# Squared activations: their sums made on GpSimd after the reload, the residual reloaded in two parts, conditioning loads given queues and slots of their own

## The chip, the cores and the metric

One core of one Trainium2 chip. The metric is the device time of one execution, in microseconds (us). Engines by their names in the profile: PE is TensorE's matmul (PEld its weight load), DVE is VectorE, ACT is ScalarE, POOL is GpSimd, SP is SyncE, whose queue issues nearly all DMAs here.

## The reference

Two transformer-like layers on x of 1024 frames by 1024 channels, fp32. Conditioning vectors come from one vector c:

```python
for layer in range(2):
    mod = silu(c) @ ada_w[layer] + ada_b[layer]          # 6 vectors of 1024
    sh1, sc1, g1, sh2, sc2, g2 = split(mod, 6)
    hn = rms_norm(h) * (1 + sc1) + sh1
    y = recurrent_mixer(hn) if layer == 0 else chunk_attention(hn, k, v)
    h = h + g1 * y
    hn = rms_norm(h) * (1 + sc2) + sh2
    h = h + g2 * (square(relu(hn @ w1)) @ w2)            # 1024 -> 4096 -> 1024
    if layer == 0:
        k, v = shared_kv(h, ...)                         # own shift and scale from c
```

## The kernel before

Activations lie transposed, channels on partitions, 1024 frames in two halves of 512. Every fp32 operand is split into a high part (a rounding copy on ScalarE) and a low part (the difference, on VectorE or GpSimd), and each product takes three matmuls (`mm3`: high by high, high by low, low by high).

The stages in order of time: start and first norm (to about 60 us), the recurrence (tiles t = 1 to 10: projections on PE, a convolution and a scan on VectorE, gates), the output projection of the mixer in three pieces of channels, MLP 0 (up 660 to 900 us, down to 1234 us), queries, keys and values (to 1520 us), attention (to 1740 us), its output projection, MLP 1 (up from about 1920 us, down from about 2180 us to the end).

Both MLPs multiply 2 by 2 blocks with seven products in place of eight (`quad`, `PROD`: B11, T1, T2, B22, T3, B21, T4). The sums of weights are four operations on GpSimd (`sums` in `add_quad`). **Up**: p = 0, 1 are done plainly, then 14 quads p = 2 to 15 of 7 x 4 x 3 = 84 matmuls; each leaves two tiles `ca`, `cb_` with the four squared blocks. `store` makes the sums T1 to T4 of these on VectorE (four operations of 128x512, two more slots) and writes eight blocks to a DRAM tensor `hid`. **Down**: 16 steps (`STEPS`): three small ones over 1, 2 and 3 of the p, then 13 full ones over four. A step needs seven operands of one new p, reloaded from `hid` and split, and four weight blocks. At the end a tail of plain products. Between up and down the residual h (8 tiles of 512 KB) is reloaded.

`Stream` feeds all weights: a list of items in order, each with loads, a split and a place: kind "w" (weights, 8 high or low tiles), kind "a" (reloaded activations, in the pool of 38 general slots) or a `use` (the 128 rows of a conditioning matrix, for which VectorE multiplies by c and sums, L235: 96 of the 112 go through the stream). All items pass one ring of 7 staging tiles `ws`, strictly in order: an item that can't be split yet holds back all behind it. `some(n)` puts n conditioning items into the list. A scheduler orders each engine's instructions in advance.

## Time and profile before

| | us |
|---|---|
| median of 3 runs | 2513.43 (2509.39 to 2513.71) |
| profiled execution, device time | 2512.36 |
| its span, first to last instruction | 2510.6 |
| PE busy | 2328.9 (93%) |
| DVE busy | 1882.3 (75%) |
| ACT busy / POOL busy | 1118.3 / 869.3 |

The device time lies 1.8 us over the span. Busy PE is not PE at its peak: a matmul's record lasts longer than its share of the pipeline, so the count of matmuls in a stretch says more than the busy time.

### The profile page before, as it was taken

What the parts mean: (1) busy time and instruction counts of PE and PEld (TensorE: products, weight loads), DVE (VectorE), ACT (ScalarE), POOL (GpSimd) and SP (SyncE); (2) the same over time, 40 slices, a digit from 0 to 9 for tenths busy, and PEclk for the clock granted to TensorE, in tenths of its full rate; (3) what the DMA queues carried; (4) which work ended last, traced back from release to release, by engine and by line L of the source; (5) the groups of instructions that cost most, each with busy time, mean ns of one, the idle gap of its engine ahead of it and who ended that gap; (6) DMA issues with size and microseconds to landing.
All of it is one profiled execution on the core that took longest, in us unless ns stands there. A gap on an engine that the chain in (4) does not pass through costs nothing.

```text
span 2510.6 us, 31957 instructions
## 1 busy us (share of the span) xinstructions
PE 2328.9 (93%) x11764; PEld 1959.8 (78%) x11764; DVE 1882.3 (75%) x2472; ACT 1118.3 (45%) x1808; POOL 869.3 (35%) x623
## 2 busy tenths in 40 slices
PE   4978997997999979999999999999999999889999
PEld 3656875875777757888899998998787888668887
DVE  8868987679777788887655465998379777777884
ACT  5466764344222234444354216998144333344441
POOL 3434445342222214232111026885044333132330
PEclk9978997998999989999999999999999999989999
DMA  7343235223565585555323400002314444755442
GB/s 292 124 138 117 72 100 180 71 84 130 193 201 191 193 286 182 182 169 189 118 60 111 142 5 12 10 20 77 143 42 151 170 170 165 258 158 160 148 151 92
DMA packets 138221, 342.50 MB, mean 136 GB/s; under 512 B 14064, under 2 KB 19312, under 8 KB 138064
## 3 DMA queue, kind: packets, MB, share of 16 engines
q1 hardware_dynamic: 136768, 336.13, 41.0%
q10 hardware_dynamic: 1296, 4.33, 0.4%
q8 instruction: 92, 1.51, 0.2%
q14 instruction: 65, 0.53, 0.1%
HBM read 244.98 MB, written 83.89 MB: 131 GB/s over the span
## 4 chain that ended last, share of the span: by engine, by line
PE 60%; DVE 19%; DMA 9%; ACT 6%; issue 5%; POOL 0%; SPq 0%; DVEq 0%; ACTq 0%; POOLq 0%
PE b L204 19%; PE b L203 19%; PE b L202 18%; DMA ws<-in_ada_dram 4%; DVE ws L235 3%; DMA ws<-in_kvada_dram 2%; DVE wl L151 2%; PE b L1250 1%; ACT s L1220 1%; DVE s L235 1%; ACT s L207 1%; DVE s L421 1%; DVE s L151 1%; PE b L1269 1%; DMA ws<-in_w_dram 1%
## 5 line engine op out<-in xcount | busy, mean ns | idle before, releaser
L203 PE MATMUL b<-s,wh 128*128 128x512 f32 x2540 | 1014.9, 400 | 57.8 <-DVE s L208 28.6
L202 PE MATMUL b<-s,wh 128*128 128x512 f32 x2540 | 1001.9, 400 | 55.5 <-ACT wh L150 22.6
L204 PE MATMUL b<-s,wl 128*128 128x512 f32 (+1 forms) x2312 | 911.8, 401 | 24.8 <-DVE wl L151 24.6
L203 PEld LDWEIGHTS b<-s,wh 128*128 128x128 f32 x2540 | 487.8, 192 | 177.1 <-DVE s L208 32.5
L202 PEld LDWEIGHTS b<-s,wh 128*128 128x128 f32 x2540 | 486.7, 192 | 175.6 <-ACT wh L150 25.0
L104 POOL TENSOR_TENSOR ws<-ws,ws 128x512 f32<-128x512 f32 (+3 forms) x180 | 290.5, 1614 | 867.6 <-DMA ws<-in_w_dram 448.1
L150 ACT ACTIVATE wh<-ws 128x1024 fp32r<-128x1024 f32 (+4 forms) x324 | 306.3, 946 | 562.9 <-PE b L204 240.8
L204 PEld LDWEIGHTS b<-s,wl 128*128 128x128 f32 (+1 forms) x2312 | 444.9, 192 | 129.5 <-DVE wl L151 31.8
L151 DVE TENSOR_TENSOR wl<-ws,wh 128x1024 fp32r<-128x1024 f32 (+3 forms) x224 | 274.9, 1229 | 143.4 <-PE b L203 72.4
L235 DVE CUSTOM_DVE_ANT_0 ws<-ws,cb,vec 128x1024 f32<-128x1024 f32 x96 | 142.9, 1490 | 158.9 <-DMA ws<-in_ada_dram 125.8
L151 DVE TENSOR_TENSOR s<-ws,s 128x512 fp32r<-128x512 f32 x230 | 193.2, 854 | 40.2 <-ACT s L150 39.8
L202 PE MATMUL b<-wh,s 128*128 128x256 f32 x768 | 217.7, 285 | 3.2 <-ACT s L396 2.0
L203 PE MATMUL b<-wl,s 128*128 128x256 f32 x768 | 217.9, 285 | 0.0
L204 PE MATMUL b<-wh,s 128*128 128x256 f32 x768 | 213.8, 285 | 3.3 <-DVE s L400 3.3
L946 DVE SCALAR_TENSOR_TENSOR s<-b,mod,s 128x512 f32<-128x512 f32 x248 | 181.8, 744 | 45.9 <-PE b L204 44.7
L150 ACT ACTIVATE s<-ws 128x512 fp32r<-128x512 f32 x230 | 138.1, 624 | 137.8 <-PE b L204 80.2
L151 POOL TENSOR_TENSOR wl<-ws,wh 128x1024 fp32r<-128x1024 f32 (+2 forms) x40 | 108.0, 2704 | 224.5 <-ACT wh L150 222.2
L202 PEld LDWEIGHTS b<-wh,s 128*128 128x128 f32 x768 | 148.8, 194 | 3.8 <-ACT s L396 2.3
L204 PEld LDWEIGHTS b<-wh,s 128*128 128x128 f32 x768 | 146.5, 194 | 4.0 <-DVE s L400 3.7
L203 PEld LDWEIGHTS b<-wl,s 128*128 128x128 f32 x768 | 148.8, 194 | 0.2 <-issue 0.2
L1225 POOL TENSOR_SCALAR s<-s,sm 128x640 f32<-128x640 f32 (+4 forms) x128 | 86.2, 685 | 22.1 <-DVE sm L1223 22.0
L104 POOL TENSOR_TENSOR ws<-ws 128x512 f32<-128x512 f32 (+3 forms) x60 | 92.2, 1536 | 0.5 <-DMA ws<-in_w_dram 0.4
(172 smaller groups left out, 3099.7 us busy)
## 6 DMA issues: line engine op xcount, KB each, us to landing
hid<-s SPq DMA_DIRECT2D x128, 512.0 KB
ws<-in_w_dram SPq DMA_DIRECT2D x216, 256.0 KB
ws<-hid SPq DMA_DIRECT2D x96, 512.0 KB
ws<-in_ada_dram SPq DMA_DIRECT2D x80, 512.0 KB
ws<-in_w_in_dram SPq DMA_DIRECT2D x22, 512.0 KB
ws<-hid SPq DMA_DIRECT2D x38, 256.0 KB
s<-in_ada_dram SPq DMA_DIRECT2D x16, 512.0 KB
hsp<-s SPq DMA_DIRECT2D x32, 256.0 KB
```

Of the source, the lines that this page charges most:

```text
L104: G.tensor_tensor(out=out, in0=in0, in1=in1, op=op)
L150: nc.scalar.activation(out=hi[:rows, :n], in_=src, func=AF.Copy)
L151: self.lo_engine.tensor_tensor(out=lo[:rows, :n], in0=src, in1=hi[:rows, :n].bitcast(F32), op=ALU.subtract)
L202: PE.matmul(ps, ah, bh, start=start, stop=False, skip_group_check=more)
L203: PE.matmul(ps, ah, bl, start=False, stop=False, skip_group_check=more)
L204: return PE.matmul(ps, al, bh, start=False, stop=stop, skip_group_check=more).ins
L207: A_.activation(out=hi, in_=src, func=AF.Copy)
L235: V.tensor_tensor_reduce(out=t, in0=t, in1=cb, op0=ALU.mult, op1=ALU.add, scale=1.0, scalar=bias, accum_out=dst)
L421: V.scalar_tensor_tensor(out=t, in0=t, scalar=self.a[:, k : k + 1], in1=self.r[:, hs(half)], op0=ALU.mult, op1=ALU.mult)
L946: V.scalar_tensor_tensor(out=t, in0=ps, scalar=g2[:, m : m + 1], in1=t, op0=ALU.mult, op1=ALU.add)
L1220: A_.activation(out=p[:, lo:640], in_=p[:, lo:640], func=AF.Exp, scale=-1.0, bias=m, accum_out=s1)
L1225: G.tensor_scalar(out=p[:, lo:640], in0=p[:, lo:640], scalar1=sm[:, 4 + e : 5 + e], scalar2=1.0, op0=ALU.mult, op1=ALU.mult)
```

## The change

**Stream**: three queues instead of one order. "w" and "a" each go on in their own order as their places come free; conditioning items are a third kind "u". Loads still stand in one order on SP; a staging tile is now given back when its own item is done, and the sums of weights may run as soon as the four blocks are there, before there is a place for the split.

**Conditioning**: `some(4)` at t = 3 to 8 of the recurrence becomes `some(2)` at t = 3 to 6 (24 items become 8), the output projection takes 16 instead of 8, and 8 move on, into MLP 0's up part, which has its 28 as before, from other vectors; queries to values take 32 instead of 24. The 28 in MLP 0's up part no longer take `ws` tiles but two slots of the general pool (`ada_late`).

**Sums of the activations**: `store` writes only `ca` and `cb_` (4 blocks instead of 8), one quad later. On reload `pair` loads two tiles, and GpSimd makes T3, T1, T2 in place once B11 and B22 are split, and T4 once B21 is.

**Residual**: h tiles 2 to 5 are reloaded during quads 8 to 11, the other four after quad 15. **Start of an MLP**: the low parts of T3 and T4 (8 per layer, `sums` of `NormS`) go from VectorE to GpSimd.

```diff
@@ Stream @@
-        self.loaded = self.split = self.pos = 0
-        self.live = {"w": 0, "a": 0}
-        self.cap = {"w": nh, "a": 0}
+        self.loaded = self.raw = self.pos = 0
+        self.queue = {"w": [], "a": [], "u": []}
+        self.live = {"w": 0, "a": 0, "u": 0}
+        self.cap = {"w": nh, "a": 0, "u": 2}
...
+    def ready(self, it, most):
+        if it["n"] >= self.loaded or (most is not None and it["n"] >= most):
+            return False
+        if it.get("need") is not None and "st" not in it["need"]:
+            return False
+        if it["after"] is not None and it["after"]["at"] < len(it["after"]["ops"]):
+            return False
+        o = it["ops"][it["at"]]
+        return callable(o) or self.live[it["to"]] + (1 if o[2] else 2) <= self.cap[it["to"]]
...
+            self.load(most)
+            for q in self.queue.values():
+                if q and self.ready(q[0], most):
+                    more = True
+                    self.step(q[0])
+                    if q[0]["at"] == len(q[0]["ops"]):
+                        q.pop(0)
@@ conditioning @@
-        some(4 if 2 < t < 9 else 0)
+        some(2 if 2 < t < 7 else 0)
...
-            some(4 if c == 1 and j > 1 else 0)
+            some(2 if c < 2 else 0)
...
-        some(3 if g > 1 else 0)
+        some(4)
@@ operands of MLP down @@
+    def pair(p):
+        x = ws.item([(0, 1024, hid[p][:, 0:2].rearrange("p a b -> p (a b)"))], [])
+        def sub(*ts):
+            def go():
+                a, b = hs(0), hs(1)
+                r0, r1 = x["st"], it["st"]
+                for t in ts:
+                    out, in0, in1 = {3: (r1[:, a], r0[:, b], r1[:, a]),
+                                     1: (r0[:, b], r0[:, b], r0[:, a]),
+                                     2: (r0[:, a], r0[:, a], r1[:, a]),
+                                     4: (r1[:, b], r1[:, b], r0[:, a])}[t]
+                    G.tensor_tensor(out=out, in0=in0, in1=in1, op=ALU.subtract)
+            return go
...
+                     [B11, B22, sub(3, 1, 2), T1, T2, T3, B21, sub(4), T4], to="a", raws=2)
@@ mlp @@
         def store(p, ca, cb_):
-            ta, tb = slot(), slot()
-            a, b = hs(0), hs(1)
-            for out, in0, in1 in ((ta[:, a], ca[:, b], ca[:, a]), (ta[:, b], ca[:, b], cb_[:, a]),
-                                  (tb[:, a], ca[:, a], ta[:, b]), (tb[:, b], cb_[:, b], tb[:, a])):
-                V.tensor_tensor(out=out, in0=in0, in1=in1, op=ALU.subtract)
-            for t, x, d in ((ca, 0, 7), (cb_, 3, 2), (ta, 1, 3), (tb, 2, 4)):
+            for t, x in ((ca, 0), (cb_, 2)):
...
-            def after(w):
+            def after(x):
+                if x == 1 and stored is not None:
+                    store(*stored)
                 if p == 15:
-                    ws.cap["a"] = (4, 8, 16, 30)[w]
+                    ws.cap["a"] = 4 * (x + 1)
                     ws.pump()
             quad([ws.next() for _ in range(4)], 4, nrm.op, read, after)
-            store(p, ca, cb_)
-        h = [slot() for _ in range(KD)]
-        for k in (2, 3, 4, 5, 6, 7, 0, 1):
-            nc.sync.dma_start(h[k], nrm.dram[k])
+            stored = (p, ca, cb_)
+            if p in (8, 9, 10, 11):
+                reload(p - 6)
+        store(*stored)
+        ws.cap["a"] = 30
+        ws.pump()
+        for k in (6, 7, 0, 1):
+            reload(k)
```

What this makes of the order, at three places. VectorE in MLP 0's up part, about one quad, before (L872 the sums of activations, L235 a conditioning multiply, which reads a `ws` tile, L151 a low part, L878 and L924 the reading of products):

```order
L151 TENSOR_TENSOR wl_5299<-ws_5094,wh_5298 128x1024
L872 TENSOR_TENSOR s_5254<-s_5120,s_5253 128x512
L924 TENSOR_TENSOR s_5263<-s_5263,b_5267 128x512
L878 SCALAR_TENSOR_TENSOR s_5263<-s_5263 128x512
L235 ISA ws_5374,kvmod<-ws_5374,cb,vec 128x1024
L235 ISA kvmod 128x1
L928 TENSOR_TENSOR s_5121<-s_5121 128x512
L872 TENSOR_TENSOR s_5254<-s_5121,s_5254 128x512
```

and in the change (L175 the low part, L274 the multiply, L947, L1000 and L1004 the reading of products):

```order
L175 TENSOR_TENSOR wl_5312<-ws_5219,wh_5311 128x1024
L274 ISA s_5349,kvmod<-s_5349,cb,vec 128x1024
L274 ISA kvmod 128x1
L274 ISA s_5352,kvmod<-s_5352,cb,vec 128x1024
L274 ISA kvmod 128x1
L1004 TENSOR_TENSOR s_5146<-s_5146 128x512
L175 TENSOR_TENSOR wl_5345<-ws_5221,wh_5344 128x1024
L1000 TENSOR_TENSOR s_5280<-s_5280,b_5283 128x512
L1000 TENSOR_TENSOR s_5280<-s_5280,b_5284 128x512
```

The sums are gone, the two multiplies of a quad stand together and read general slots. GpSimd in MLP 1's down part, the full steps, before (L104 the sums of weights, four to a step):

```order
L104 TENSOR_TENSOR ws_18997<-ws_19007,ws_18918 128x512
L104 TENSOR_TENSOR ws_18918<-ws_19007 128x512
L104 TENSOR_TENSOR ws_18958<-ws_18997,ws_19007 128x512
L104 TENSOR_TENSOR ws_18958<-ws_18997,ws_18958 128x512
L104 TENSOR_TENSOR ws_19147<-ws_19157,ws_19068 128x512
```

and in the change (L111 the sums of weights, L359 those of activations):

```order
L111 TENSOR_TENSOR ws_18703<-ws_18725,ws_18602 128x512
L111 TENSOR_TENSOR ws_18602<-ws_18725 128x512
L111 TENSOR_TENSOR ws_18666<-ws_18703,ws_18725 128x512
L111 TENSOR_TENSOR ws_18666<-ws_18703,ws_18666 128x512
L359 TENSOR_TENSOR ws_18747<-ws_18728,ws_18747 128x512
L359 TENSOR_TENSOR ws_18728<-ws_18728 128x512
L359 TENSOR_TENSOR ws_18728<-ws_18728,ws_18747 128x512
L359 TENSOR_TENSOR ws_18747<-ws_18747,ws_18728 128x512
L111 TENSOR_TENSOR ws_18853<-ws_18875,ws_18752 128x512
```

A full step has eight operations instead of four. SP's queue where MLP 1 goes from up to down, before (L874 stores, L118 stream loads, L940 the residual):

```order
L874 DMA hid<-s_17923 128x2x512
L940 DMA s_17935<-hsp_15013 128x1024
L940 DMA s_17936<-hsp_15013 128x1024
L940 DMA s_17937<-hsp_15013 128x1024
L940 DMA s_17938<-hsp_15013 128x1024
L940 DMA s_17939<-hsp_15013 128x1024
L874 DMA hid<-s_17768 128x2x512
L940 DMA s_17940<-hsp_15013 128x1024
L940 DMA s_17933<-hsp_15013 128x1024
L874 DMA hid<-s_17924 256x1x512
L940 DMA s_17934<-hsp_15013 128x1024
L118 DMA ws_17968<-hid 128x512
```

and in the change (L944, L137, L987):

```order
L944 DMA hid<-s_17530 128x1024
L137 DMA ws_17755<-hid 128x1024
L137 DMA ws_17769<-hid 128x1024
L137 DMA ws_17777<-in_w_dram 128x512
L987 DMA s_17717<-hsp_14885 128x1024
L987 DMA s_17719<-hsp_14885 128x1024
L987 DMA s_17721<-hsp_14885 128x1024
L987 DMA s_17723<-hsp_14885 128x1024
L137 DMA ws_17806<-in_w_dram 128x512
```

Four of the eight reloads are gone from this place, and they stand behind the operands of the third small step instead of ahead of them. Of the conditioning multiplies ahead of MLP 0, VectorE's order had 24 in the first half of the recurrence and 8 behind; it now has 8 there and then 16, the 16 of the output projection, which are drawn forward into the last four tiles of the recurrence.

## Rows read from the trace of the kernel before

**Rows 1.** The page: its head, and its first part (busy time of each engine, share of the span, instructions).
```profile
span 2510.6 us, 31957 instructions
PE 2328.9 (93%) x11764; PEld 1959.8 (78%) x11764; DVE 1882.3 (75%) x2472; ACT 1118.3 (45%) x1808; POOL 869.3 (35%) x623
```

**Rows 2.** Busy time of each engine by stretch: the stretch and its length, PE, PEld, DVE, ACT, POOL with their instructions, granted clock of PE, DMA share, GB/s.
```profile
60.00:250.00 190.00, 160.19 (x621) 122.17 (x620) 149.60 (x147) 106.61 (x128) 80.84 (x32) 0.87 0.40 124
250.00:480.00 230.00, 211.16 (x868) 165.82 (x867) 195.34 (x137) 142.51 (x157) 113.07 (x40) 0.93 0.36 108
480.00:660.00 180.00, 156.67 (x653) 125.69 (x652) 138.31 (x174) 66.99 (x106) 49.93 (x30) 0.93 0.35 118
660.00:891.00 231.00, 215.24 (x924) 174.51 (x923) 169.04 (x210) 65.86 (x93) 58.17 (x42) 0.99 0.59 194
891.00:960.00 69.00, 53.45 (x207) 40.01 (x206) 57.83 (x85) 25.92 (x45) 16.97 (x14) 0.90 0.84 287
960.00:1234.00 274.00, 273.12 (x1205) 225.11 (x1204) 211.22 (x271) 107.71 (x152) 81.20 (x50) 1.00 0.53 170
1234.00:1520.00 286.00, 279.50 (x2291) 277.95 (x2291) 159.29 (x199) 99.74 (x202) 42.80 (x30) 0.99 0.25 78
1920.00:2162.00 242.00, 242.00 (x1069) 200.37 (x1069) 185.24 (x198) 76.22 (x108) 78.45 (x50) 1.00 0.48 164
2162.00:2220.00 58.00, 42.04 (x147) 31.29 (x145) 43.12 (x62) 19.62 (x35) 12.03 (x11) 0.82 0.77 270
2220.00:2460.00 240.00, 239.59 (x1049) 197.94 (x1050) 194.46 (x230) 101.04 (x141) 82.82 (x50) 0.99 0.50 153
```

**Rows 3.** ACT in order of time, the reading of a quad's last product (L927) of two quads in MLP 0, ten apart, and of two in MLP 1, eleven apart: start, duration, engine and line, idle time before.
```profile
657.56 0.60 ACT L927 ACTIVATE s<-b 128x512 f32<-128x512 f32 x1 [7.94 <-PE b L204]
870.00 0.60 ACT L927 ACTIVATE s<-b 128x512 f32<-128x512 f32 x1 [5.56 <-PE b L204]
...
1931.36 0.60 ACT L927 ACTIVATE s<-b 128x512 f32<-128x512 f32 x1 [3.59 <-PE b L204]
2140.80 0.60 ACT L927 ACTIVATE s<-b 128x512 f32<-128x512 f32 x1 [3.58 <-PE b L204]
```

**Rows 4.** VectorE's waits in 660 to 891 us: who waited for whom, us in total, times, longest.
```profile
DVE ws L235 <- DMA ws<-in_kvada_dram: 32.9, 12, 3.9
DVE ws L235 <- DMA ws<-in_ada_dram: 21.6, 8, 3.0
```

**Rows 5.** The chain that ended last, in order of time, in one quad of MLP 0: start, duration, what.
```profile
718.00 4.75 DMA ws<-in_ada_dram
722.77 1.28 DVE ws L235
724.09 4.17 DMA ws<-in_ada_dram
```

**Rows 6.** VectorE's waits in 60 to 250 us (columns as in rows 4).
```profile
DVE ws L235 <- DMA ws<-in_ada_dram: 31.8, 14, 5.9
```

**Rows 7.** PE's waits in 60 to 250 us.
```profile
PE b L203 <- DVE s L208: 20.6, 4, 11.7
PE b L202 <- ACT s L207: 7.8, 2, 4.0
```

**Rows 8.** PE's waits in 2162 to 2220 us, MLP 1's crossing from up to down.
```profile
PE b L202 <- ACT wh L150: 8.4, 2, 6.0
PE b L204 <- DVE wl L151: 3.9, 2, 3.1
```

**Rows 9.** GpSimd in order of time there: the first sums of weights of the third small step, with the idle time before.
```profile
2198.34 1.01 POOL L104 TENSOR_TENSOR ws<-ws,ws 128x384 f32<-128x384 f32 x1 [17.93 <-DMA ws<-in_w_dram]
```

**Rows 10.** Groups by line with shapes kept apart: line, engine, operation, shapes, count, busy us, mean ns of one, idle before.
```profile
L235 DVE CUSTOM_DVE_ANT_0 ws<-ws,cb,vec 128x1024 f32<-128x1024 f32 x96 | 142.9, 1490 | 158.9 <-DMA ws<-in_ada_dram 125.8 <-DMA ws<-in_kvada_dram 33.0
L872 DVE TENSOR_TENSOR s<-s,s 128x512 f32<-128x512 f32 x96 | 81.6, 850 | 2.0
L872 DVE TENSOR_TENSOR s<-s 128x512 f32<-128x512 f32 x32 | 33.7, 1053 | 0.9
L427 POOL TENSOR_TENSOR s<-s,s 128x512 fp32r<-128x512 f32 x16 | 23.8, 1499 | 34.3 <-ACT s L426 30.0 <-PE b L204 4.4
L444 DVE TENSOR_TENSOR s<-s,s 128x512 fp32r<-128x512 f32 x32 | 22.6, 746 | 0.0
```

**Rows 11.** GpSimd in order of time in one full step of MLP 1's down part, its four sums of weights.
```profile
2323.57 1.76 POOL L104 TENSOR_TENSOR ws<-ws,ws 128x512 f32<-128x512 f32 x1 [13.28 <-DVE s L946]
2325.29 1.29 POOL L104 TENSOR_TENSOR ws<-ws 128x512 f32<-128x512 f32 x1
2326.53 3.54 POOL L104 TENSOR_TENSOR ws<-ws,ws 128x512 f32<-128x512 f32 x2
```

**Rows 12.** VectorE in the same stretch.
```profile
2323.49 0.68 DVE L151 TENSOR_TENSOR s<-ws,s 128x512 fp32r<-128x512 f32 x1
2324.51 0.75 DVE L946 SCALAR_TENSOR_TENSOR s<-b,mod,s 128x512 f32<-128x512 f32 x1 [0.33 <-PE b L204]
2327.70 1.23 DVE L151 TENSOR_TENSOR wl<-ws,wh 128x1024 fp32r<-128x1024 f32 x1 [2.44 <-ACT wh L150]
2328.84 2.38 DVE L151 TENSOR_TENSOR s<-ws,s 128x512 fp32r<-128x512 f32 x2
2331.15 0.74 DVE L946 SCALAR_TENSOR_TENSOR s<-b,mod,s 128x512 f32<-128x512 f32 x1
```

More of the change, by code (lines that the diff above doesn't have):

```diff
@@ new lines, in ready, with step, tile @@
+    def ready(self, it, most):
[7 more added lines that the diff above has]
+        return callable(o) or self.live[it["to"]] + (1 if o[2] else 2) <= self.cap[it["to"]]
+    def step(self, it):
+        nc = self.nc
+        st, rows, to = it["st"], it["rows"], it["to"]
+        o = it["ops"][it["at"]]
+        it["at"] += 1
+        if callable(o):
+            o()
+        else:
+            def tile(what):
+                if to == "a":
+                    return self.slot(F32R)
+                return self.wp.tile([128, 1024], F32R, name=f"{what}{it['n']}", tag="wh")
+            c0, n, one = o
+            hi = tile("wh")
+            if one:
+                hi, lo = hi[:, 0:n], hi[:, n : 2 * n]
+            else:
+                lo = tile("wl")
+            if "of" in it and c0 < 1024:
+                st = it["of"]["st"]
+            src = st[:rows, c0 % 1024 : c0 % 1024 + n]
+            nc.scalar.activation(out=hi[:rows, :n], in_=src, func=AF.Copy)
+            self.lo_engine.tensor_tensor(out=lo[:rows, :n], in0=src,
+                                         in1=hi[:rows, :n].bitcast(F32), op=ALU.subtract)
+            it["op"].append((hi, lo))
+            it["hi"], it["lo"] = it["op"][0]
+            self.live[to] += 1 if one else 2
+        if it["at"] == len(it["ops"]):
+            if it["raw"] == "ws":
+                self.raw -= it["raws"]
+            else:
+                self.live["u"] -= 1
@@ L160, in next @@
+    def pump(self, most=None):
+        more = True
+        while more:
+            more = False
+            self.load(most)
+            for q in self.queue.values():
+                if q and self.ready(q[0], most):
+                    more = True
+                    self.step(q[0])
+                    if q[0]["at"] == len(q[0]["ops"]):
+                        q.pop(0)
     def next(self):
-        while self.items[self.pos]["use"] is not None or self.items[self.pos]["to"] != "w":
+        while self.items[self.pos]["to"] != "w" or not self.items[self.pos]["ops"]:
@@ L295, in mlp_units @@
             ws.add(I["w1"][l][f], 1024)
+        late = []
         for q in range(2, 16):
             u, v = I["w1"][l][2 * q], I["w1"][l][2 * q + 1]
-            ws.add_quad(u[:, :512], u[:, 512:], v[:, :512], v[:, 512:], 512)
-            some(2)
+            its = ws.add_quad(u[:, :512], u[:, 512:], v[:, :512], v[:, 512:], 512)
+            for it in late:
+                it["after"] = its[1]
+            late = ada_late(2)
         for j, p0, p1 in STEPS:
@@ L302, in mlp_units @@
             c = slice(p0 * 128, p1 * 128)
-            at = len(ws.items)
-            ws.add_quad(*(I["w2"][l][j][x][:, c] for x in range(4)), n)
-            hs_ = []
-            for x in range(4):
-                parts = [(0, HALF, True), (HALF, HALF, True)] if x < 3 else [(0, HALF, True)]
-                w = sum(n_ for _, n_, _ in parts)
-                hs_.append(ws.item([(0, w, hid[p1 - 1][:, 2 * x : 2 * x + w // HALF].rearrange(
-                    "p a b -> p (a b)"))], parts, to="a"))
-            ws.items[at:] = [it for two in zip(ws.items[at : at + 4], hs_) for it in two]
-            hitems[l, p1 - 1] = hs_
+            its = ws.add_quad(*(I["w2"][l][j][x][:, c] for x in range(4)), n)
+            for it in late:
+                it["after"] = its[1]
+            late = []
+            hitems[l, p1 - 1] = pair(p1 - 1)
             if j:
@@ L318, in mlp_units @@
             p = 13 + t
[L319 removed]
+            hitems[l, p, "B12"] = ws.item([(0, HALF, hid[p][:, 1])], [(0, HALF, True)], to="a")
     mlp_units(0)
@@ L492, in quad @@
                 ws.done(it)
-                after(w)
+            after(x)
     def tail(its, body, nrm):
@@ L912, in mlp, with reload @@
                 store(f // 2, *hk[f // 2])
+        h = [None] * KD
+        def reload(k):
+            h[k] = slot()
+            nc.sync.dma_start(h[k], nrm.dram[k])
+        stored = None
         for p in range(2, 16):
```

128 lines of the change are left out of this document (65 added, 63 removed).

## Prediction

> **What bounds the kernel now.** I read the page first: 2510.6 us of span, and the device time of the same execution, 2512.4 us, is what the sum below is made against [rows 1]; it lies 1.1 us under the median of the runs. Then the busy times by stretch, because 93% of PE is an average. MLP 1's up part shows what a full PE is: 1069 matmuls in 242.0 us, 0.2264 us each, at a granted clock of 1.00 [rows 2]. With this yardstick each stretch has a loss, its length less its matmuls times 0.2264: 49 us in 60 to 250, 34 in 250 to 480, 32 in 480 to 660, 22 in MLP 0's up part (660 to 891), 22 and 25 at the two crossings from up to down (891 to 960, 2162 to 2220), but only 1 and 3 in the two down parts [rows 2]. The change can win only where a loss stands, and can lose where PE is full today.
>
> Next, why. A quad of MLP 0 takes 21.24 us (212.4 over ten), one of MLP 1 takes 19.04 (209.4 over eleven) [rows 3]. The two parts differ by the conditioning rows alone. In MLP 0 VectorE stands 54.5 us before conditioning multiplies whose data isn't there [rows 4], and the chain of work runs through two such loads in series in each quad: 4.75 us of load, 1.28 of multiply, 4.17 of load [rows 5]. The ring of seven tiles makes this: the load can't start before an older item leaves. The recurrence shows the same: 31.8 us of such waits in 60 to 250 us [rows 6], while PE waits there 28.4 us for splits that stand behind them on VectorE and ScalarE [rows 7]. At the crossing of MLP 1, without conditioning, PE waits for weight splits [rows 8], and these for sums on GpSimd, which idled 17.9 us until a weight block had landed [rows 9]; the DMA share is 0.77 there and 0.84 in MLP 0 [rows 2]. So the crossings are short of loads first, and of VectorE second (57.8 busy of 69 us in MLP 0) [rows 2].
>
> **The change, term by term.**
>
> *MLP 0's up part, 22 us won.* The conditioning loads get two slots and a queue of their own. A pair is used once a quad, so its successor is under way for most of 19 us, against some 9 us of load [rows 5]: VectorE should find it landed. The four sums per quad leave too, 0.85 us each [rows 10]. What hides the rest is what hides it in MLP 1: no stall at 1069 matmuls in 242 us [rows 2]. Bounds: 0 (if SP's order holds the loads back) and 22.
>
> *Crossings, 20 of 47 us won.* Gone are half of the reload (2 MB of some 16 to 20 MB that the stretch moves by its rate and length [rows 2], about 7 us each), half of the blocks stored, and eight sums on VectorE, 6.8 us [rows 10]. Against that stand the new sums on GpSimd, dear here as the next paragraphs show. I take 10 us at each. Bounds 0 and 40.
>
> *The recurrence, 12 won.* Ahead, 16 multiplies fewer at 1.49 us [rows 10] and 31.8/24 = 1.33 of wait [rows 6]: 45 us off VectorE's queue in a stretch where PE lost 49 and waited 28 for splits [rows 2, 7]. I take 22. The 8 that are added and those drawn forward come in the second half, where VectorE is busy 195 of 230 us and PE loses less [rows 2]: 8 x 2.8 = 23 us more on VectorE, of which I charge 10. Bounds -10 and 35.
>
> *Start of both MLPs, 3 won.* VectorE loses 8 low parts at 0.75 us and the 8 sums of p = 0 and 1 per layer; GpSimd gains 8 operations at 1.5 us [rows 10]. Bounds -4 and 10.
>
> *Queries to values, nothing.* Eight more multiplies, 23 us with their waits, lie beside a PE that is busy 279.5 of 286 us, on a VectorE idle for 127 [rows 2]. If this cover failed, about 5 us.
>
> *Full down steps, 22 lost.* This is the dispute. GpSimd has four sums in a step; it gets eight. By busy time nothing speaks against it: 82.8 of 240 us would become about 166 [rows 2]. But look at single operations. GpSimd's sums follow each other every 1.24 us when alone (2325.29 to 2326.53); the one at 2323.57 takes 1.76, just as long as VectorE's low part, begun 0.08 us before it, needed to end; and the last two take 3.54 instead of 2.5, because VectorE's low part of 1.14 us falls between them [rows 11, 12]. In return VectorE's two low parts at 2328.84 take 2.38 us: they begin to run only at 2330.07, when GpSimd ends [rows 11, 12]. The adds out of PSUM are 0.75 and 0.74 us, beside GpSimd or not [rows 12]. So a VectorE operation with both inputs in SBUF and a GpSimd sum take turns, a whole instruction each. In turns, a full step has 8 x 0.60 + 3 x 1.14 = 8.2 us of VectorE's low parts (0.54 to 0.68 us for a short one [rows 12]) and 8 x 1.24 = 9.9 of GpSimd: 18.1 us of 19.0 that PE needs for 84 matmuls. Today it is 13.2. In MLP 0 nine of the 13 full steps have a conditioning multiply besides, both inputs in SBUF, 1.28 us [rows 5]: 19.4, more than PE's time. On top VectorE must make seven adds of 0.67 us, and GpSimd can only use these if it has work ready. The trace shows no stretch so full of turns, so I bound it: nothing (GpSimd fills every gap of VectorE, and operands are made a step ahead), to 2.5 us a step (GpSimd's four new sums of 1.24, half of them in VectorE's way). I take 0.6 us for the 17 steps without and 1.3 for the 9 with a multiply: 10 + 12.
>
> The Trainium skill's GPSIMD Engine Reference, section Key points, says that the engine shares its SBUF interfaces with VectorE and contends with VectorE instructions that have two SBUF inputs. The trace agrees (2.38 us against two of 0.68 or less). Its section Engine selection puts two-input sums on VectorE, since GpSimd is about two times slower for them. Here it is 1.24 against 0.60. By that rule the change would lose in the down parts; by busy shares it would cost nothing there.
>
> The crossing feels the turns too. Three small steps are 126 matmuls, 28.5 us. In turns they need 21 low parts, 12.6, weights' low parts about 6, 12 sums of activations, 14.9, and of weights about 7.4: 41 us, 45 with MLP 0's multiplies. Only since this can begin during quad 15 does it fit into 28.5 + 19.0, with little to spare. Hence 20 and not 40.
>
> Sum: 22 + 20 + 12 + 3 - 22 = 35 us, 2512.4 - 35 = 2477.
>
> **Rivals.** *The turns cost nothing and the crossings heal* (27%): 22 + 38 + 12 + 3 gives about 2437. For it: GpSimd idles for 13.28 us in each step today [rows 11], sums of weights may now run early, the operands a step ahead. Against: 18.1 of 19.0.
>
> *The turns bound the down parts* (12%): full steps of 21.5 us, 65 us over 26 steps, and no gain at the crossings: 2512 - 22 - 12 - 3 + 65 = 2540, slower. It decides from 57/26 = 2.2 us a step on, 21.2 us. For it: MLP 0's steps are over 19.0 by turns alone, and what GpSimd is late by, the next low part is late by. Against: VectorE idled 2.44 us in the step shown [rows 12], which GpSimd could use.
>
> *The loads don't come free* (16%): SP issues everything in one order, and a load that waits for one of the 38 slots holds up weights behind it; a late quad takes all of them (28 operands, four for `ca` and `cb_`, four reloaded tiles, two for conditioning). Then MLP 0's quads stay near 21.2 us and the second wave of the recurrence costs 20: 35 - 22 - 10 leaves 3, about 2509.
>
> **How the numbers follow.** My own case, 2477, has 45% and a range of 2460 to 2495. For 8 in 10 I need the bulk of the first rival and the third: 2430 to 2520; left out are the faster end of the first, some 10%, and most of the second, some 9%. A difference of 0.2%, 5 us, is about what a measurement of this kernel can tell from no change. Faster: 45 + 27 + about half of the third, 80%. Within 0.2%: 7%. Slower: 13%, the turns and the rest of the third.
>
> **What would show it.** L1004 (the last product's reading) every 19.0 us in MLP 0's up part, and few waits of L274 for loads there: the first term. The crossings: as forecast, 10 us won at each put some 44 more matmuls into stretches of the same length, 251 instead of 207 and 191 instead of 147. Full down steps of 19.6 us in MLP 1 and up to 20.3 in MLP 0, with low parts of VectorE at 1.0 us or more on average and GpSimd's sums at 1.7 or more: the turns. In the recurrence, fewer waits of VectorE before 250 us and more after. The time comes out below the forecast if the down steps stay at 19.0 us, and above it if they pass 21.

## The result, and the profile after

The changed kernel takes 2516.34 us (median, 2509.70 to 2523.19) against 2510.55 for the kernel before (17 runs each): ratio 1.0026, 95% interval 1.0017 to 1.0036. It is no faster, a little slower; the forecast was 2477 us. The profiled execution took 2512.75 us.

The head of the page of the changed kernel and its busy times (compare [rows 1]), then busy time by stretch (columns as in [rows 2]):

```profile
span 2511.0 us, 31516 instructions
PE 2323.5 (93%) x11764; PEld 1941.9 (77%) x11764; DVE 1821.6 (73%) x2328; ACT 1114.5 (44%) x1808; POOL 1112.0 (44%) x767
```
```profile
60.00:250.00 190.00, 173.09 (x720) 134.99 (x718) 158.37 (x127) 121.22 (x146) 90.92 (x36) 0.94 0.31 91
250.00:480.00 230.00, 200.95 (x803) 157.29 (x801) 182.97 (x145) 128.03 (x140) 101.45 (x37) 0.88 0.39 118
660.00:864.00 204.00, 202.87 (x895) 167.70 (x895) 142.74 (x176) 65.64 (x94) 71.16 (x46) 1.00 0.50 173
891.00:960.00 69.00, 63.97 (x266) 50.25 (x267) 64.75 (x69) 26.16 (x38) 47.13 (x29) 0.98 0.37 119
960.00:1234.00 274.00, 245.84 (x1075) 194.60 (x1073) 197.95 (x243) 94.55 (x139) 130.04 (x79) 1.00 0.38 125
2162.00:2220.00 58.00, 51.20 (x208) 37.36 (x206) 51.61 (x59) 25.12 (x39) 42.24 (x27) 1.00 0.46 152
2220.00:2460.00 240.00, 220.25 (x937) 174.97 (x936) 178.01 (x208) 85.31 (x126) 137.94 (x89) 0.99 0.33 105
```

PE is full in MLP 0's up part (895 matmuls in 204 us, 0.228 us each) and has gained at both crossings (266 for 207, 208 for 147). It has lost in both down parts: 1075 for 1205 and 937 for 1049, at a granted clock of 1.00 and 0.99, as before. VectorE is busy there 72% and 74% of the time, GpSimd 47% and 57%, the DMA engines 38% and 33%. None of these is busy all the time, and yet PE waits.

Fixed events give the balance. ScalarE's reading of MLP 0's last product of a quad, ten quads apart (compare [rows 3]), and VectorE's add that ends the third small step and the last full step, for each MLP, before (L946) and after (L1027):

```profile
633.06 0.60 ACT L1003 ACTIVATE s<-b 128x512 f32<-128x512 f32 x1 [4.30 <-PE b L243]
827.76 0.60 ACT L1003 ACTIVATE s<-b 128x512 f32<-128x512 f32 x1 [3.84 <-PE b L243]
```
```profile
955.84 0.74 DVE L946 SCALAR_TENSOR_TENSOR s<-b,mod,s 128x512 f32<-128x512 f32 x1
1200.97 1.41 DVE L946 SCALAR_TENSOR_TENSOR s<-b,mod,s 128x512 f32<-128x512 f32 x2
2229.77 0.74 DVE L946 SCALAR_TENSOR_TENSOR s<-b,mod,s 128x512 f32<-128x512 f32 x1
2474.86 1.41 DVE L946 SCALAR_TENSOR_TENSOR s<-b,mod,s 128x512 f32<-128x512 f32 x2
```
```profile
907.13 0.74 DVE L1027 SCALAR_TENSOR_TENSOR s<-b,mod,s 128x512 f32<-128x512 f32 x1
1191.43 0.75 DVE L1027 SCALAR_TENSOR_TENSOR s<-b,mod,s 128x512 f32<-128x512 f32 x1 [4.18 <-PE b L243]
2201.86 0.73 DVE L1027 SCALAR_TENSOR_TENSOR s<-b,mod,s 128x512 f32<-128x512 f32 x1
2477.72 0.75 DVE L1027 SCALAR_TENSOR_TENSOR s<-b,mod,s 128x512 f32<-128x512 f32 x1 [4.18 <-PE b L243]
```

A quad of MLP 0 takes 19.47 us (194.70 over ten; 21.24 before). In us, the starts of such readings and the ends of such adds (the lead is before less after):

| event | before | after | lead | won since the last |
|---|---|---|---|---|
| MLP 0, first quad read | 634.2 | 618.4 | 15.8 | 15.8 |
| last quad read | 902.4 | 863.6 | 38.7 | 22.9 |
| third small step done | 956.6 | 907.9 | 48.7 | 10.0 |
| last full step done | 1202.4 | 1192.2 | 10.2 | -38.5 |
| MLP 1, last quad read | 2173.2 | 2162.6 | 10.6 | 0.4 |
| third small step done | 2230.5 | 2202.6 | 27.9 | 17.3 |
| last full step done | 2476.3 | 2478.5 | -2.2 | -30.1 |

What was won, 66 us, went back in the 26 full steps: 68.6 us. A step took 18.9 us in both MLPs; it takes 21.9 in MLP 0 and 21.2 in MLP 1.

How one such step runs, by the chain of work that ended last, in order of time (start, duration, what; short pieces left out):

```profile
2302.38 1.85 DVE wl L175
2304.25 5.67 DMA ws<-hid
2310.00 0.64 ACT s L174
2310.66 0.70 DVE s L175
2311.43 1.31 POOL ws L359
2312.81 2.16 POOL ws L359
2315.04 1.31 POOL ws L359
2316.37 0.64 ACT s L174
...
2318.30 1.29 DVE s L175 x2
2319.73 1.30 POOL ws L359
2321.06 0.64 ACT s L174
...
2322.33 1.23 DVE wl L175
2323.58 4.61 DMA ws<-hid
```

A pair of tiles is loaded, its second block split, three sums made, these split, the fourth sum made and split, and after a weight block's low part, which gives a staging tile back, the next pair is loaded: 19.3 us from load to load here, with no PE in it. Over 2225 to 2440 us, ten steps, the same groups lead the chain (its shares by line, the head of the row; 4.0% are PE's):

```profile
by line: DMA ws<-hid 26.7%; POOL ws L359 21.5%; DVE s L175 13.1%; issue 7.6%; ACT s L174 6.5%; POOL ws L111 6.0%; DVE s L1027 5.9%; DVE wl L175 4.8%; DVE wh L175 2.4%; PE b L241 1.4%; PE b L243 1.3%; PE b L242 1.3%; ACT wh L174 1.1%; SPq L1
```

PE itself waits mostly for adds out of PSUM there (who waits for whom, us, times, longest); these stand in VectorE's order among the low parts, for which VectorE waits 54.3 us:

```profile
PEld b L241 <- DVE s L1027: 16.8, 16, 2.3
PE b L241 <- DVE s L1027: 11.9, 11, 1.9
```

SP's queue of the same kernel shows the rhythm (start, time until the last issue), and then what it waited for in 2225 to 2440 us:

```profile
2303.16 1.41 SPq L137 DMA_DIRECT2D ws<-hid  x2
2305.94 15.91 SPq L137 DMA_DIRECT2D ws<-in_w_dram  x4
2322.44 1.46 SPq L137 DMA_DIRECT2D ws<-hid  x2
2325.37 18.01 SPq L137 DMA_DIRECT2D ws<-in_w_dram  x4
2343.47 0.86 SPq L137 DMA_DIRECT2D ws<-hid  x2
```
```profile
SPq L137 <- DVE wl L175: 118.1, 25, 10.9
SPq L137 <- POOL ws L359: 55.4, 11, 9.3
```

Four weight loads are drawn out over 16 to 18 us, and the next pair stands behind them. SP waits for staging tiles that the low parts of weights give back, and once a step for the one that the fourth sum gives back.

### The profile page after: what moved, and what is told of

The parts are those of the page before. It is cut to its first block, busy times and chain, and to the rows that moved or that the text cites. A ratio compares the mean times of both kernels' runs of the same rounds, so it can differ in the third digit from the quotient of the medians.

```text
span 2511.0 us, 31516 instructions
## 1 busy us (share of the span) xinstructions
PE 2323.5 (93%) x11764; PEld 1941.9 (77%) x11764; DVE 1821.6 (73%) x2328; ACT 1114.5 (44%) x1808; POOL 1112.0 (44%) x767
## 4 chain that ended last, share of the span: by engine, by line
PE 48%; DVE 22%; DMA 9%; ACT 8%; POOL 7%; issue 6%; SPq 0%; POOLq 0%; DVEq 0%; ACTq 0%
PE b L242 15%; PE b L243 14%; PE b L241 14%; DMA ws<-hid 5%; POOL ws L359 5%; DVE s L175 4%; DMA ws<-in_ada_dram 2%; DVE wl L175 2%; DVE s L1027 2%; POOL ws L111 2%; DVE ws L274 2%; ACT s L174 1%; PE b L1334 1%; ACT s L1304 1%; DVE s L274 1%
## 5 line engine op out<-in xcount | busy, mean ns | idle before, releaser
L111 POOL TENSOR_TENSOR ws<-ws,ws 128x512 f32<-128x512 f32 (+3 forms) x180 | 283.1, 1573 | 489.0 <-DMA ws<-in_w_dram 277.9
L175 DVE TENSOR_TENSOR wl<-ws,wh 128x1024 fp32r<-128x1024 f32 (+3 forms) x224 | 301.4, 1348 | 110.5 <-PE b L242 54.9
L175 DVE TENSOR_TENSOR s<-ws,s 128x512 fp32r<-128x512 f32 x230 | 199.2, 885 | 137.8 <-ACT s L174 137.0
L359 POOL TENSOR_TENSOR ws<-ws,ws 128x512 f32<-128x512 f32 x96 | 153.1, 1595 | 131.0 <-DVE s L175 128.5
L1027 DVE SCALAR_TENSOR_TENSOR s<-b,mod,s 128x512 f32<-128x512 f32 x248 | 181.4, 741 | 37.1 <-PE b L243 37.1
L175 POOL TENSOR_TENSOR wl<-ws,wh 128x1024 fp32r<-128x1024 f32 (+2 forms) x40 | 106.2, 2660 | 218.0 <-ACT wh L174 218.0
L274 DVE CUSTOM_DVE_ANT_0 ws<-ws,cb,vec 128x1024 f32<-128x1024 f32 x68 | 101.8, 1501 | 94.9 <-DMA ws<-in_ada_dram 94.9
L274 DVE CUSTOM_DVE_ANT_0 s<-s,cb,vec 128x1024 f32<-128x1024 f32 x44 | 79.2, 1826 | 36.1 <-DMA s<-in_ada_dram 31.0
```

The lines of the kernel that those rows point to most:

```text
L111: G.tensor_tensor(out=out, in0=in0, in1=in1, op=op)
L175: self.lo_engine.tensor_tensor(out=lo[:rows, :n], in0=src, in1=hi[:rows, :n].bitcast(F32), op=ALU.subtract)
L274: V.tensor_tensor_reduce(out=t, in0=t, in1=cb, op0=ALU.mult, op1=ALU.add, scale=1.0, scalar=bias, accum_out=dst)
L359: G.tensor_tensor(out=out, in0=in0, in1=in1, op=ALU.subtract)
L1027: V.scalar_tensor_tensor(out=t, in0=ps, scalar=g2[:, m : m + 1], in1=t, op0=ALU.mult, op1=ALU.add)
```

## The experiments

Three theories. **Turns**: VectorE and GpSimd exclude each other, the prediction's price and its slower rival. **Chain**: one pair of activations at a time goes through load, sums and splits, since its tiles come back only after T4 (at first put down to the ring of seven, "ring", as the first expectations call it). **Order**: the queues as such. The table has the mean of the 13 full steps (third small step's end to last full step's end; * the first 12, where MLP 0's last one is disturbed by rows moved behind it). Each ratio is against runs of the kernel before that were made beside it (medians 2509.86 to 2511.72 us).

| kernel | us | ratio, 95% interval | MLP 0 | MLP 1 |
|---|---|---|---|---|
| before | 2510.55 | | 18.91 | 18.91 |
| changed | 2516.34 | 1.0026 (1.0017 to 1.0036) | 21.87, 22.25* | 21.22 |
| e4 sums ahead of the store | 2480.36 | 0.9875 (0.9858 to 0.9891) | 19.06 | 18.85 |
| e3 before + extra sums, MLP 1 | 2521.44 | 1.0040 (1.0025 to 1.0055) | 18.95 | 19.70 |
| e1 sums on VectorE | 2496.21 | 0.9938 (0.9924 to 0.9953) | 20.66 | 20.84 |
| e2 nine staging tiles | 2526.45 | 1.0058 (1.0043 to 1.0073) | 20.57 | 19.95 |
| e5 two own slots for a pair | 2533.86 | 1.0090 (1.0075 to 1.0105) | 21.31 | 21.54 |
| e6 the same, sums on VectorE | 2502.55 | 0.9973 (0.9962 to 0.9984) | 20.64 | 19.69 |
| e10 pair ahead of the weights | 2513.65 | 1.0010 (0.9997 to 1.0023) | 21.70 | 20.79 |
| e8 four slots, two pairs | 2499.46 | 0.9954 (0.9938 to 0.9969) | 20.80, 21.13* | 19.53 |
| e9 the same, sums on VectorE | 2483.88 | 0.9890 (0.9870 to 0.9909) | 20.15, 20.46* | 19.15 |
| e14 changed, rows elsewhere | 2507.54 | 0.9987 (0.9977 to 0.9997) | 21.65* | 21.49 |
| e16 e8, rows elsewhere | 2488.36 | 0.9910 (0.9896 to 0.9925) | 19.92* | 19.49 |
| e15 e9, rows elsewhere | 2468.47 | 0.9837 (0.9816 to 0.9858) | 19.29* | 18.95 |

**The sums ahead of the store again (e4).** `store` as before with four sums on VectorE and eight blocks, four items per p on reload, the residual in one part; queues and conditioning as changed.

```diff
-            for t, x in ((ca, 0), (cb_, 2)):
+            ta, tb = slot(), slot()
...
+                V.tensor_tensor(out=out, in0=in0, in1=in1, op=ALU.subtract)
+            for t, x, d in ((ca, 0, 7), (cb_, 3, 2), (ta, 1, 3), (tb, 2, 4)):
...
-            hitems[l, p1 - 1] = pair(p1 - 1)
...
+            ws.items[at:] = [it for two in zip(its, hs_) for it in two]
...
+            hitems[l, p1 - 1] = hs_
```

> The changed kernel with the old way of the activations: VectorE makes the sums ahead of the store, eight blocks are stored and reloaded in four items, and the residual is reloaded in one part. The queues and slots for conditioning, the moved conditioning items and the low parts on GpSimd at the start of the MLPs stay. All theories but 'order': down steps return to 18.9 us, the lead of 15.8 us at the first quad and 23 in MLP 0's up part stays, the crossings are as before (no gain of 10 and 17): 2512 - 39 = 2473, 2465 to 2482. 'Order' (the three queues hold PE up in the down parts): steps stay at 21 us, 2525 or more.

The steps are back at 19.06 and 18.85 us, the time at 2480, as all theories but "order" had it. The loss comes with the moved sums and the pair; "order" in its wide form is out. The run also tells what freed MLP 0's up part. Its quads take 19.04 us (190.40 over ten), less than the changed kernel's 19.47, with the four sums still on VectorE:

```profile
643.25 0.60 ACT L993 ACTIVATE s<-b 128x512 f32<-128x512 f32 x1 [3.58 <-PE b L243]
833.65 0.60 ACT L993 ACTIVATE s<-b 128x512 f32<-128x512 f32 x1 [3.59 <-PE b L243]
```

So the queues and slots of the conditioning loads are enough for that; the moved sums were not needed.

**GpSimd's work without its chain (e3).** The kernel before, MLP 1 only:

```diff
+                if l == 1 and p1 - p0 == 4 and x > 2:
+                    m, half = spots[x]
+                    G.tensor_tensor(out=cb[:, hs(0)], in0=cb[:, hs(0)], in1=h[m][:, hs(half)],
+                                    op=ALU.subtract)
```

> The kernel before, with four extra subtractions of 128x512 on GpSimd in each of the 13 full down steps of MLP 1, each after one of the last four adds of the step; they write a tile that nobody reads any more, so no load, split or release waits for them. GpSimd and VectorE then have the instructions of the changed kernel's step (eight sums on GpSimd), without its chain. 'Turns': the 13 steps go from 18.9 us to 21 or more, the time from 2511 to 2535 or more, MLP 0 unchanged. 'Ring': the 13 steps stay at 18.9 to 19.3 us, the time within 5 us of 2511.

In between the two answers: 19.70 us, 0.8 a step, and 2521 us. Low parts of the activations by shape, before and with the extra sums, both over some ten steps of MLP 1 (count, busy, mean ns, idle before):

```profile
L151 DVE TENSOR_TENSOR s<-ws,s 128x512 fp32r<-128x512 f32 x70 | 63.3, 911 | 19.4 <-ACT s L150 19.3
```
```profile
L151 DVE TENSOR_TENSOR s<-ws,s 128x512 fp32r<-128x512 f32 x71 | 78.1, 1115 | 11.8 <-ACT s L150 11.8
```

The turns are there (0.2 us more for each low part) and PE pays for some of it. The 0.8 us is probably an upper bound for the turns, since the extra sums also stand ahead of weight sums in GpSimd's queue; that is argued, not shown. The changed kernel, whose steps are 1.5 us longer still, shows less of them:

```profile
L175 DVE TENSOR_TENSOR s<-ws,s 128x512 fp32r<-128x512 f32 x73 | 64.0, 891 | 54.7 <-ACT s L174 54.3
L359 POOL TENSOR_TENSOR ws<-ws,ws 128x512 f32<-128x512 f32 x31 | 47.7, 1539 | 42.4 <-DVE s L175 41.6
```

Its low parts of activations are no longer than before (0.891 us; those of weights are, 1.476 for 1.318), but VectorE stands 54.7 us before them. That is waiting more than turns. A long low part is no sign of a long step either: in the settled steps of e8 below, where PE is full, they take 1.023 us:

```profile
L176 DVE TENSOR_TENSOR s<-s,s 128x512 fp32r<-128x512 f32 x42 | 42.5, 1023 | 11.3 <-ACT s L175 11.3
```

**The sums on VectorE at the reload (e1)**, in `sub`:

```diff
-                    G.tensor_tensor(out=out, in0=in0, in1=in1, op=ALU.subtract)
+                    V.tensor_tensor(out=out, in0=in0, in1=in1, op=ALU.subtract)
```

> The changed kernel with the four sums T1 to T4 of the reloaded activations on VectorE instead of GpSimd; everything else stays. In the changed kernel a full down step takes 21.9 us on average in MLP 0 and 21.2 in MLP 1, before it took 18.9 (26 steps, 68.6 us in all). Theory 'turns' (VectorE's two-SBUF-input operations and GpSimd's sums exclude each other, a whole instruction each): a step's turns fall from 18.1 us to 8 x 0.60 + 4 x 0.60 + 3 x 1.14 + 4 x 1.24 = 15.6, so steps of 19.0 to 19.8 us and a time of 2445 to 2465. Theory 'ring' (load of a pair, split, sums, split, release of its two staging tiles, next load, one after the other through seven staging tiles): the four sums get about 1.0 us shorter each (mean 1.60 now), the loop falls from 21.6 to about 17.6 us, under what PE needs, so steps of 19.0 to 19.5 and the same time. Theory 'order' (the two-part reload and the three queues themselves hold PE up, whoever makes the sums): steps stay at 21 us or more and the time at 2500 or more.

All three miss: 2496 us. "Turns" and "ring" wanted steps of 19.0 to 19.8 us; they fall by 1.2 and 0.4 us only, to 20.66 and 20.84. GpSimd is a small part of it.

**Nine staging tiles (e2).**

```diff
-    ap_ = ctx.enter_context(tc.tile_pool(name="ap", bufs=38))
+    ap_ = ctx.enter_context(tc.tile_pool(name="ap", bufs=36))
-    wsp = ctx.enter_context(tc.tile_pool(name="wsp", bufs=7))
+    wsp = ctx.enter_context(tc.tile_pool(name="wsp", bufs=9))
...
-    ws = Stream(nc, whp, wsp, slot, 8, 7)
+    ws = Stream(nc, whp, wsp, slot, 8, 9)
```

> The changed kernel with nine staging tiles instead of seven; the room comes from the general slots, 36 instead of 38. 'Ring': the next pair of activations is loaded while the last one is still being summed, full down steps fall from 21.2 and 21.9 us to 19.0 to 20.0, and the time to 2450 to 2480, less what two missing general slots cost elsewhere (shown by the stages ahead of the down parts). 'Turns': GpSimd and VectorE have the same instructions to share, steps stay at 21.2 to 21.9 us and the time at 2505 to 2520.

With GpSimd's work unchanged the steps of MLP 1 fall to 19.95 us on average; after the first two they take 18.8 to 19.6 until the last two. Those of MLP 0, 20.57 us, stay above the 20.0 of "ring". The time is worse all the same: the first quad of MLP 0 is read at 631.5 us instead of 618.4. The recurrence loses these 13 us; that the 36 general slots cost them, and not the two staging tiles more, was not tested. The waits tell what went. ScalarE in the changed kernel (2225 to 2440) and here (2280 to 2470; who waits for whom, us, times, longest); its waits for loads of activations are gone:

```profile
ACT s L174 <- POOL ws L359: 78.0, 25, 6.6
ACT s L174 <- DMA ws<-hid: 55.3, 18, 6.1
```
```profile
ACT s L174 <- POOL ws L359: 95.6, 27, 5.7
POOL ws L359 <- DVE s L175: 46.1, 11, 5.0
DVE s L175 <- ACT s L174: 32.7, 20, 3.7
```

**Two slots of its own for a pair (e5), also with sums on VectorE (e6).** The ring is for weights alone; room comes from operands made ahead, 28 instead of 30.

```diff
-        self.cap = {"w": nh, "a": 0, "u": 2}
+        self.cap = {"w": nh, "a": 0, "u": 2, "p": 0}
...
-            "p a b -> p (a b)"))], [])
+            "p a b -> p (a b)"))], [], raw="p")
...
-                    ws.cap["a"] = 4 * (x + 1)
+                    ws.cap["a"], ws.cap["p"] = 4 * x + 2, 2
```

> The changed kernel, where the two reloaded tiles of a pair of activations no longer stand in the ring of seven staging tiles but in two general slots of their own; at most 28 split operands instead of 30, so that the 38 slots suffice. The ring is then for weights (and the few conditioning rows of the down part) alone. GpSimd still makes all sums. 'Ring': loads of activations leave before the weights of the step are split, full down steps fall from 21.9 and 21.2 us to 19.0 to 20.0 in both layers, the crossings stay, and the time is 2516 less 40 to 60: 2450 to 2480. 'Turns': GpSimd and VectorE have the same instructions, 0.8 us a step by the run with extra sums as the least; if they are the cause of the rest, steps stay at 21 us and the time at 2505 or more.

> The same with two slots for the pair, and the four sums on VectorE instead of GpSimd. If what is left after the slots are given is turn-taking, steps fall to 19.0 us, some 10 to 20 us in all under the run with slots alone. If VectorE's queue is the limit (four sums more of 0.6 us stand ahead of adds that PE waits for), steps are equal or longer, as in the run with the sums on VectorE alone, where steps took 20.7 us.

By the numbers the answer of "turns" comes true in e5 (21 us or more, over 2505), but e8 below refutes it. "Ring" as I had put it falls: seven tiles are free for weights, and the steps stay at 21.3 and 21.5 us. The crossings, which should have stayed, take 50.0 and 51.4 us instead of 44.3 and 40.0, and that is why the time rose to 2534. A pair still has but two places, so one pair at a time goes through. How that holds the step is not settled by the trace: in 2245 to 2460 us SP waits 173.2 us for tiles that the low parts of weights give back and 0.9 us for the pair's sums. But those low parts stand in VectorE's order among others that wait for the pair's sums.

With the shorter sums of VectorE (e6) the steps shorten, to 20.6 and 19.7 us, not to the 19.0 forecast; the time falls by 31 us, more than the 10 to 20 forecast.

**The pair ahead of the weights in SP's order (e10).**

```diff
+            hitems[l, p1 - 1] = pair(p1 - 1)
             its = ws.add_quad(*(I["w2"][l][j][x][:, c] for x in range(4)), n)
...
-            hitems[l, p1 - 1] = pair(p1 - 1)
```

> The changed kernel with one thing turned round: in the list of each down step the pair of activations stands ahead of the step's four weight blocks, not behind, so SP issues its loads first. Seven staging tiles as in the changed kernel. If the loads of activations are late because they queue behind loads of weights that wait for a staging tile, steps fall below 20.5 us and the time to 2500 or less. If it is the number of tiles and the pair's own chain, whichever stands first, steps stay at 21 to 22 us, the time at 2510 to 2520.

The time and MLP 0 (21.7 us) are as the second answer has it, MLP 1 (20.8) lies between. Standing behind weights costs 0.2 and 0.4 us a step.

**Two pairs in flight (e8), also with sums on VectorE (e9).** Four slots for pairs, 26 operands; since a full step needs 28, its operands are looked up one product at a time:

```diff
-                    ws.cap["a"], ws.cap["p"] = 4 * x + 2, 2
+                    ws.cap["p"] = 2 if x < 2 else 4
+                    ws.cap["a"] = 4 * (x + 1) - ws.cap["p"]
...
-        ws.cap["a"] = 28
+        ws.cap["a"] = 26
...
-            mov = {}
...
+            class mov:
...
+                    return it["op"][it["names"].index(key[0])]
```

> As the run with two slots for a pair, but with four, so that the next pair is loaded while the last is still being summed; at most 26 split operands, so that the 38 general slots suffice. With one pair in flight its chain (load 5.4 us, two splits, three sums between weight sums, splits, the fourth sum, its split, release) came back every 21.4 us. Theory 'one pair at a time': two in flight take the chain off the path, full steps fall from 21.4 to 19.0 to 20.0 us as they did with nine staging tiles (19.4 in MLP 1), the time is 2534 less 40: 2480 to 2500. 'Turns' (VectorE and GpSimd have too much to share): steps stay at 21 us, 2525 or more.

> The same four slots with the four sums on VectorE. If with two pairs in flight turn-taking is what is left (0.8 us a step by the run with extra sums), steps fall to 19.0 us and the time by 10 to 20 us against the run with four slots alone. If VectorE's own queue is then the limit, steps are as long or longer.

The missing place for a second pair is the cause. Against e5 the run has two slots more for pairs, two places fewer for operands and the late lookup. The lookup was not tested alone, but e2, which keeps it as it was, gained in the same way in its settled steps. MLP 1 comes to 19.53 us, with GpSimd's eight sums in every step, and in its settled steps the chain that ended last (here 2310 to 2332 us of e8, shares by line; shares of overlapping pieces can pass 100%) is PE alone:

```profile
by line: PE b L244 35.6%; PE b L242 33.2%; PE b L243 32.0%
```

Those steps take 19.3 us with GpSimd's sums and 18.9, some 19.9, with VectorE's. MLP 0, 20.80 us, misses the 20.0 forecast; the next runs say why. The time of e9 is 15.6 us under e8's, as forecast. So of MLP 1's 30.1 us, 22.0 are the one pair at a time (21.22 less 19.53, 13 times), 4.9 the sums on GpSimd (19.53 less 19.15), 3.2 remain.

**The conditioning rows of MLP 0 (e14, e16, e15).** MLP 0 kept 1.3 and 1.0 us a step more than MLP 1 with two pairs. The 12 rows of its down part go behind it:

```diff
-            if j:
-                some(1)
...
             ws.add(I["wq"][g * 2 + kk], 1024)
+        some(6 if g < 2 else 0)
```

> The changed kernel, where the 12 conditioning rows that stood in MLP 0's down part (nine of them in full steps) go among the query weights behind it. 'Rows': MLP 0's full steps (21.9 us) become like MLP 1's (21.2 us), 9 us won in the down part, 2516 becomes 2508 to 2515 with what the rows cost in the queries. 'Not the rows': steps stay at 21.9 us.

> The kernel with four slots for two pairs in flight, sums on GpSimd, and the 12 rows among the query weights. 'Rows': MLP 0's full steps fall from 20.8 to MLP 1's 19.5 us, 17 us won, 2499 becomes 2482 to 2490. 'Not the rows': they stay over 20.4 us.

> The same with the sums on VectorE. 'Rows': MLP 0's full steps fall from 20.2 to 19.2 us, 13 us won, 2484 becomes 2471 to 2477. 'Not the rows': they stay over 19.9 us.

The rows are that rest: 7 us over 12 steps in the changed kernel, 14 to 15 with two pairs, and the first 12 steps of the two MLPs are then within 0.2 us of each other. MLP 0's last step gives 4 to 6 us of it back (20.99 us in e16 for 16.81 in e8, 23.42 in e14 for 17.27). e14 and e15 come out just under their ranges, e16 within. e15 has the lowest median here, 1.6% under before; e17's interval overlaps with its own.

**The residual in one part (e13)**, the changed kernel:

```diff
-            if p in (8, 9, 10, 11):
-                reload(p - 6)
...
-        for k in (6, 7, 0, 1):
+        for k in (2, 3, 4, 5, 6, 7, 0, 1):
```

> The changed kernel with the residual reloaded in one part after quad 15, as before; nothing else undone. It tells how much of the crossings' gain (from the last quad's reading to the end of the third small step 54.2 us became 44.3, and 57.3 became 40.0) is the reload's. By the term of the prediction, half of the reload at each crossing, some 7 us: 50 to 52 and 47 to 50 us, and a time of 2521 to 2531. If VectorE, busy 50 of 50 us there, sets the crossing, both stay within 3 us and the time at 2510 to 2520.

2542.99 us (ratio 1.0127, 1.0108 to 1.0145). From the last quad's reading to the third small step the crossings take 55.1 and 51.8 us (before 54.2 and 57.3) instead of 44.3 and 40.0: 22.6 of the 27.3 us won there are the reload's, more than the 7 us each that the forecast gave it. Both answers miss the time; some 4 us more go between the MLPs (732.2 us for 728.0). e4, whose residual comes in one part too, crosses in 48.4 and 46.2 us: the moved sums cost each crossing 5 to 7 us. The reload stands in the chain that ended last of the kernel before (902 to 958 us, a row that the view cuts off; in the changed kernel's, 864 to 908 us, it does not appear):

```profile
by line: issue 22.7%; DVE s L151 15.1%; DMA s<-hsp 14.3%; DMA ws<-in_w_dram 10.3%; DMA ws<-in_kvada_dram 7.0%; POOL ws L104 7.0%; DVE s L946 5.8%; DVE wl L151 4.7%; PE b L204 4.2%; DMA ws<-hid 3.7%; ACT wh L150 3.4%; PE b L203 2.9%; PE b L2
```

**Conditioning back in its old places (e7)**, on e4:

```diff
-        some(2 if 2 < t < 7 else 0)
+        some(4 if 2 < t < 9 else 0)
...
-            some(2 if c < 2 else 0)
+            some(4 if c == 1 and j > 1 else 0)
...
-        some(4)
+        some(3 if g > 1 else 0)
```

> The kernel with the old way of the activations (sums ahead of the store), and the conditioning items back in their old places: 24 in the recurrence, 8 in the output projection, 24 in queries to values. It shows what the moved items are worth alone. By the prediction's term (22 won early, 10 given back) 12 us: 2480 becomes 2490 to 2495, the first quad of MLP 0 is read at 630 to 634 us instead of 620. If the lead comes from the queues and slots (no item holds back weights behind it), the time stays at 2478 to 2484.

2485.89 us (0.9899, 0.9885 to 0.9914). The first quad is read at 631.0 us instead of 620.4, so the places are worth 10.6 us there. Only 5.5 are left at the end, so the time lies between the two answers: from the end of MLP 0 to the start of MLP 1's quads e4 is 8 us slower, with eight more rows between queries and values.

**Better kernels on e4 (e12, e17).** Residual tiles 2 and 3 reloaded early; then the 12 rows elsewhere too.

```diff
             store(p, ca, cb_)
+            if p in (12, 13):
+                reload(p - 10)
```

> The kernel with the old way of the activations (2480 us), with the two tiles of the residual that the first small step needs reloaded during quads 12 and 13, the other six after quad 15. In that kernel PE stands 11.1 and 9.6 us at the two crossings before a product whose bank waits for an add, and the add for the residual (7.3 and 8.0 us of load in the chain). If that is the path, 8 to 11 us are won at each crossing: 2460 to 2465. If weights and low parts are as late (VectorE is busy 47 of 52 us there), 0 to 4 us each: 2472 to 2480.

> The kernel with the sums ahead of the store and two residual tiles reloaded early (2475 us), with the 12 rows among the query weights. Its full steps in MLP 0 take 19.2 to 19.6 us on average against 18.9 in MLP 1, so 'rows' expects 4 to 6 us less, 2469 to 2473; 'not the rows' expects no change.

2474.66 (0.9858, 0.9843 to 0.9872) and 2472.29 us (0.9847, 0.9832 to 0.9861). The crossings shrink from 48.4 and 46.2 to 42.0 and 36.8 us in e12, but the next steps give part back (24.0 us for the first in MLP 0), and the time is the second answer's. In e17 the first 12 steps of MLP 0 fall from 19.7 to 18.9 us and the last takes 26.1; the 2.4 us between the two times are not clear of the noise.

## Why the prediction was wrong

- **MLP 0's up part, 22 forecast: 22.9.** Right in its main reason, the loads: VectorE still waits 21.9 us for them there (54.5 in [rows 4]), but PE is full, and by e4 also with the sums on VectorE. That the number fits so well is in part luck: ten quads give 17.7 us, the first gives 8.7 and the last two take 3.5 back.
- **Recurrence 12 and heads 3, 15 forecast: 15.8.** Right in sign and shape, in the sum partly by luck. 60 to 250 us holds 99 matmuls more ([rows 2]), 22.4 us as forecast; 250 to 480 holds 65 fewer, 14.7 us against 10. The other 8 us come after 480 us, of which the forecast said only the 3 of both MLPs' starts. e7 shows 10.6 for the places of the rows alone.
- **Crossings, 20 forecast: 27.3.** Right in sign, low in size. The cause I named first, the reload, is the one, but it is worth 11 us a crossing and not 7: e13 takes 22.6 back. Against it stands the cost of the moved sums, which I had named without a price.
- **Queries to values, nothing: 0.4.** So in the changed kernel, from MLP 0's last step to MLP 1's last quad; e4, with the same rows, lost 8 us between the MLPs against e7. Why the one and not the other is open.
- **Full down steps, 22 forecast: 68.6.** The step that failed. I priced GpSimd's new sums as a share of a common interface, 0.6 or 1.3 us a step, bounds 0 to 2.5; the steps grew by 2.64 on average, outside. The turns themselves were priced about right: e8 against e9 gives 0.4 us a step, e3 0.8. The conditioning rows add 0.6 to 1.2 in MLP 0; whether by turns or by their staging tile was not told apart. What the sum put at nothing is latency. The changed `pair` ties seven operands to two tiles given back only when T4 is split, and puts two groups of GpSimd sums with two handovers each between load and release. I read "operands are made a step ahead" as cover; but there is a place for one pair only, and 5.7 us of load, 4.9 of three sums, 1.3 of the fourth and the splits, adds and weights' low parts between make 19.3 us in series in the piece shown, 21.0 from the next load to the one after, against the 19.0 that PE needs. With two pairs in flight (e8) MLP 1's steps came to 19.53 us. The prediction walked such a loop for conditioning in [rows 5] and did not walk it for the pair.
- **The slower rival** (steps of 21.5 us, "the turns bound the down parts") had the steps' length and the wrong cause. The prediction named a check for the turns, low parts of 1.0 us and GpSimd's sums of 1.7 or more. It was a poor one: low parts are 0.89 us for activations and 1.48 for weights, the new sums 1.54, and e8 with a full PE has low parts of 1.02. The crossings without gain were wrong too.
- **The third rival** has a time, 2509, close to the measured one, by luck: its quads near 21.2 us did not come.

The Trainium skill's page "SBUF — State Buffer", section "SBUF: two separate sides", calls the pair of ports that VectorE and GpSimd share an exclusive lock for the whole instruction. The traces agree in direction: with the extra sums of e3 low parts take 1.115 us on average for 0.911. The Trainium skill's GPSIMD Engine Reference, section Engine selection, puts two-input sums on VectorE, since GpSimd is about two times slower. The comparison of e8 and e9 agrees, by 16 us.

What stays open: by which path one pair at a time holds the step in e5, the 3.2 us that MLP 1's steps take longer in e9 than before, and the 8 us of e4 between the MLPs.
